# Indexer scores: two 64-row matmuls in the two halves of the array in place of two 128-row matmuls that are half zero

## Chip, cores and metric

The kernel runs on one NeuronCore of one Trainium2 chip. The metric is the device time of one execution in microseconds (us); before the change it is the median of three runs.

## What is computed

Two layers of a hybrid block on 512 tokens of width 2048. The even layer is a convolution branch beside block attention. The odd layer is an attention in which an indexer chooses the keys: for every query it scores all earlier keys with 16 small heads of 64 dimensions, and only the 128 keys with the highest scores are attended to. The part that matters here:

```python
idx = jnp.einsum('bqhd,bsd->bqhs', iq_c, ik)          # 16 heads, 64 dimensions
score = jnp.einsum('bqhs,bqh->bqs', jax.nn.relu(idx), iw_c)
score = jnp.where(kpos[None, :] <= qpos[:, None], score, -jnp.inf)
sel = lax.top_k(score, k_top)[1]                      # k_top = 128
```

## The kernel before, in words

Products are computed to nearly float32 accuracy with rounded operands: each operand is split into a high part (the value rounded to the fast matmul format, by ScalarE) and a low part (the remainder, by VectorE), and a product is the sum of high x high, high x low and low x high. `mm3` (L80 to L89) issues these three matmuls; `gemm` (L118 on) uses it for every projection, with weights that arrive by DMA in pieces and are split as they come. The work of all engines is ordered ahead of time by a planner, from the program order, due times set by `at`, and a simulated timeline.

The odd layer (`odd`, L618 on) first computes the latent queries and keys and the indexer's key `ik` (64 dimensions, 512 keys). `ik` is copied to the upper 64 partitions too, so that each half of the partitions holds it once. From it come four tiles of 128 partitions: `ihl` has the high part in the lower half and the low part in the upper half, `ilh` the other way round, `h0` has the high part below and zeros above, `zh` zeros below and the high part above (L645 to L654).

Then the 16 heads are worked off in 8 pairs. One `gemm` (L671, 384 query columns, the first 128 queries need no selection) gives the queries of two heads, one in each half of the partitions. For each head, `iq` gets the head's high part in its own half and its low part in the other half (L677, L678). For each of three chunks of 128 queries there are two matmuls into one PSUM bank, with `iq` as the weights and the keys as 256, 384 or 512 moving columns: L685 multiplies high by low and low by high in one matmul over all 128 rows, L686 multiplies high by high, with the zeros of `h0` or `zh` against the half that holds the low part. ScalarE takes the bank out with a relu (L688), and VectorE adds it, times the head's weight, into the score tile of the chunk (L690, L692). The five PSUM banks of the tags `s` and `x` are taken in turn.

After three projections ahead of the loop, four more (`gate`, L658 to L664, 16 k-steps of three matmuls) run among the head pairs, and the rest after them, while VectorE selects the 128 highest scores (L697 to L713). The attention that follows uses the selection (L238).

`colsum` (L161 to L169) sums over partitions with a matmul against ones; it is called with 64 rows and 64 columns for the indexer key's normalization.

Of the kernel before, what the change touches and what calls it, by code (L numbers as in the profile page):

```python
# [7 lines left out]
F32R = mybir.dt.float32r  # L8
I32 = mybir.dt.int32
AF = mybir.ActivationFunctionType  # L10
# [4 lines left out]
P = 128  # L15
T = 512
NT = T // P
# [9 lines left out]
KTOP = 128  # L27
# [12 lines left out]
def f32(ap):  # L40
    return ap.bitcast(F32)


class Builder:
# [573 lines left out]
    def odd(self):  # L618
        nc, d = self.nc, self.d
# [8 lines left out]
        px = self.psum("x")  # L628
# [3 lines left out]
        ik = self.s("C")  # L632
# [11 lines left out]
        lo, hi = slice(0, DI), slice(DI, P)  # L644
        ilh, ihl = self.s("T", dt=F32R), self.s("T", dt=F32R)  # L645
# [1 line left out]
        nc.scalar.activation(ilh[hi, :], ik[hi, :], AF.Copy)  # L647
        nc.vector.tensor_tensor(ilh[lo, :], ik[lo, :], f32(ihl[lo, :]), op=OP.subtract)
        nc.vector.tensor_tensor(ihl[hi, :], ik[hi, :], f32(ilh[hi, :]), op=OP.subtract)
        h0, zh = self.s("T", dt=F32R), self.s("T", dt=F32R)  # L650
        nc.vector.memset(f32(h0[hi, :]), 0.0)
        nc.vector.memset(f32(zh[lo, :]), 0.0)
        nc.scalar.activation(h0[lo, :], ik[lo, :], AF.Copy)
        nc.scalar.activation(zh[hi, :], ik[hi, :], AF.Copy)  # L654

        gates = []

        def gate():  # L658
            n = len(gates)
            ps = self.gemm(d["w_in2"][6 + n], self.xs)  # L660
            g = self.s("Y")
            nc.vector.tensor_tensor(g, ps, self.r, op=OP.mult)
            nc.scalar.activation(g, g, AF.Silu)
            gates.append(g)  # L664
# [4 lines left out]
        for i in range(HI // 2):  # L669

            ps = self.gemm(d["w_iq"][i], [(a[:, KTOP:], b[:, KTOP:]) for a, b in cq], n=T - KTOP)  # L671
            for e in range(2):
                h = 2 * i + e
                own, other = (lo, hi) if e == 0 else (hi, lo)
                iq = self.s("C", dt=F32R)
                n = T - KTOP
                nc.scalar.activation(iq[own, :n], ps[own, :n], AF.Copy)  # L677
                nc.vector.tensor_tensor(iq[other, :n], ps[own, :n], f32(iq[own, :n]), op=OP.subtract)  # L678
                cross, main = (ilh, h0) if e == 0 else (ihl, zh)
                for c in range(1, NT):  # L680
                    w = P * (c + 1)
                    cs = slice(c * P - KTOP, (c + 1) * P - KTOP)

                    px = self.psum("s" if (3 * h + c) % 5 < 2 else "x")
                    nc.tensor.matmul(px[:, :w], iq[:, cs], cross[:, :w], start=True, stop=False)  # L685
                    nc.tensor.matmul(px[:, :w], iq[:, cs], main[:, :w], start=False, stop=True)  # L686
                    rl = self.s("tmp" if (3 * h + c) % 2 else "u")
                    nc.scalar.activation(rl[:, :w], px[:, :w], AF.Relu)  # L688
                    if h == 0:
                        nc.vector.tensor_scalar(sc[c][:, :w], rl[:, :w], iw[:, c, h:h + 1], None, op0=OP.mult)  # L690
                    else:
                        nc.vector.scalar_tensor_tensor(sc[c][:, :w], rl[:, :w], iw[:, c, h:h + 1], sc[c][:, :w],  # L692
                                                       op0=OP.mult, op1=OP.add)
            self.t += 2
            if i < GI:
                gate()
# [25 lines left out]
        for pair in range(HO // 2):  # L722
# [5 lines left out]
            for b in range(2):  # L728
                ps = self.psum("g")
                for a in range(2):  # L730
                    c = 2 * b + a
                    for k in range(2):
                        cs = slice(c * P, (c + 1) * P)
# [6 lines left out]
            for e in range(2):  # L740
                h = 2 * pair + e
                th = t0 + D * e + (0 if e else 2.6)
                parts = []
                for i, (w, xs, o) in enumerate(((wk, ckv, 256 * e), ((wq0, wq1)[e], cq, 0))):
# [5 lines left out]
                    zh, zl = self.s("A2", dt=F32R), self.s("A2", dt=F32R)  # L750
# [6 lines left out]
                k, q = parts  # L757
# [159 lines left out]
```

## Time and profile before

| | |
|---|---|
| median of 3 runs | 1522.16 us (1520.82 to 1522.37) |
| profiled execution | 1521.33 us |
| its span, first to last instruction | 1519.5 us |
| mean granted TensorE clock | 0.996 |
| TensorE matmul busy | 1504.2 us, 99% of the span |
| VectorE busy | 1018.8 us, 67% |
| ScalarE busy | 677.5 us, 45% |

The span lies inside the profiled execution's time; what surrounds it is 1.8 us. The engines are named PE (TensorE matmul), PEld (TensorE weight load), DVE (VectorE), ACT (ScalarE), POOL (GpSimd) and SP (SyncE). Matmuls are pipelined and the ends of their records are modelled, so what a matmul costs is read from the start of one to the start of the next. A tile is written as weights' rows * columns, and then the moving operand.

### The profile page before, as it was taken

How to read it: one execution, taken by the hardware profiler on the slowest of the kernel's cores; microseconds unless marked ns; L12 is line 12 of the kernel's file. 1: busy time of each engine (PE TensorE's matmuls, PEld its weight loads, DVE VectorE, ACT ScalarE, POOL GpSimd, SP SyncE). 2: the span in 40 equal slices, each digit the busy share in tenths (PEclk: the TensorE clock that was granted, in tenths of full speed). 3: DMA queues.
4: the chain of work that ended last, by engine and by line, in shares of the span. 5: the costliest groups of instructions: out<-in, count | busy, mean ns of one | idle time of the engine just before them, and what ended most of it. 6: DMA issues, size and time to landing. Idle time of an engine off the chain costs nothing.

```text
span 1519.5 us, 20122 instructions
## 1 busy us (share of the span) xinstructions
PE 1504.2 (99%) x7137; PEld 1261.3 (83%) x7137; DVE 1018.8 (67%) x1980; ACT 677.5 (45%) x1219; POOL 55.5 (4%) x117
## 2 busy tenths in 40 slices
PE   9999999999999999999999999999999999999996
PEld 7888888888888888888888887788888889888886
DVE  7799999976576645664444445557995898843344
ACT  7533333345374534543333333545324666633341
POOL 0000000002022202220000000000000000000000
PEclk9999999999999999999999999999999999999998
DMA  7233333356234733364444332222232111133333
GB/s 234 89 105 114 102 106 102 104 146 173 93 108 132 204 104 115 113 173 138 146 145 145 125 98 85 95 91 78 90 98 91 55 51 49 56 125 118 126 125 112
DMA packets 97397, 173.22 MB, mean 114 GB/s; under 512 B 12112, under 2 KB 18000, under 8 KB 97296
## 3 DMA queue, kind: packets, MB, share of 16 engines
q1 hardware_dynamic: 93280, 164.45, 34.5%
q0 software_dynamic: 3584, 7.35, 1.7%
q8 instruction: 56, 0.92, 0.2%
q14 instruction: 45, 0.37, 0.1%
q10 hardware_dynamic: 432, 0.14, 0.0%
HBM read 153.93 MB, written 10.49 MB: 108 GB/s over the span
## 4 chain that ended last, share of the span: by engine, by line
PE 97%; DMA 1%; DVE 1%; ACT 0%; issue 0%; SPq 0%; DVEq 0%; ACTq 0%
PE psg L87 28%; PE psg L89 28%; PE psg L88 28%; PE psx L87 1%; PE psx L88 1%; PE psx L89 1%; PE psx L249 1%; PE pss L88 1%; PE pss L89 1%; PE pss L87 1%; PE pso L88 1%; PE pso L89 1%; PE pso L87 1%; DMA wr<-in_w_v 1%; DMA C<-in_w_in 0%; PE psx L686 0%
## 5 line engine op out<-in xcount | busy, mean ns | idle before, releaser
L96 ACT ACTIVATE wh<-wr 128x512 fp32r<-128x512 f32 x508 | 319.4, 629 | 652.2 <-PE psg L89 542.1
L97 DVE TENSOR_TENSOR wl<-wr,wh 128x512 fp32r<-128x512 f32 x508 | 348.5, 687 | 296.3 <-ACT wh L96 295.4
L87 PE MATMUL psg<-A,wh 128*128 128x512 f32 (+1 forms) x1328 | 517.0, 390 | 0.2 <-DVE tmp L782 0.2
L88 PE MATMUL psg<-A,wl 128*128 128x512 f32 x1120 | 436.5, 390 | 0.0
L89 PE MATMUL psg<-A,wh 128*128 128x512 f32 x1120 | 436.4, 390 | 0.0
L87 PEld LDWEIGHTS psg<-A,wh 128*128 128x128 f32 (+1 forms) x1328 | 248.7, 187 | 52.8 <-ACT wh L96 0.6
L88 PEld LDWEIGHTS psg<-A,wl 128*128 128x128 f32 x1120 | 209.6, 187 | 44.8 <-issue 0.4
L89 PEld LDWEIGHTS psg<-A,wh 128*128 128x128 f32 x1120 | 209.6, 187 | 44.4 <-issue 0.4
L415 DVE SCALAR_TENSOR_TENSOR C<-u,cst,C 128x512 f32<-128x512 f32 x240 | 170.0, 745 | 0.2
L89 PE MATMUL psg<-Y,wh 128*128 128x512 f32 x336 | 130.9, 390 | 0.0
L88 PE MATMUL psg<-Y,wl 128*128 128x512 f32 x336 | 130.9, 390 | 0.0
L290 POOL DMA_DIRECT2D turn<-turn x112 | 55.0, 499 | 609.0 <-DVE turn L286 459.4
L88 PEld LDWEIGHTS psg<-Y,wl 128*128 128x128 f32 x336 | 63.0, 188 | 13.0
L89 PEld LDWEIGHTS psg<-Y,wh 128*128 128x128 f32 x336 | 63.1, 188 | 12.8
L87 PE MATMUL psg<-T,wh 128*128 128x512 f32 x160 | 62.6, 391 | 0.0
L88 PE MATMUL psg<-G,wl 128*128 128x512 f32 (+1 forms) x160 | 60.7, 379 | 0.0
L89 PE MATMUL psg<-G,wh 128*128 128x512 f32 (+1 forms) x160 | 60.6, 379 | 0.0
L87 PE MATMUL psg<-Y,wh 128*128 128x512 f32 x128 | 49.8, 389 | 0.0
L240 ACT ACTIVATE C<-C,col 128x128 f32<-128x128 f32 (+1 forms) x64 | 35.8, 560 | 15.6 <-DVE col L238 15.2
L87 PE MATMUL psg<-G,wh 128*128 128x512 f32 (+1 forms) x96 | 36.2, 377 | 0.0
L87 PEld LDWEIGHTS psg<-T,wh 128*128 128x128 f32 x160 | 30.0, 188 | 6.1 <-DVE A L97 0.2
L89 PEld LDWEIGHTS psg<-G,wh 128*128 128x128 f32 x160 | 30.1, 188 | 5.1
(316 smaller groups left out, 2137.0 us busy)
## 6 DMA issues: line engine op xcount, KB each, us to landing
wr<-in_w_in SPq DMA_DIRECT2D x268, 256.0 KB, 3.0
wr<-in_w_out SPq DMA_DIRECT2D x128, 256.0 KB, 2.9
wr<-in_w_v SPq DMA_DIRECT2D x64, 256.0 KB, 2.9
wr<-in_w_qk SPq DMA_DIRECT2D x32, 256.0 KB, 2.4
turn<-turn POOLq DMA_DIRECT2D x112, 64.0 KB, 3.9
Y<-in_xT SPq DMA_DIRECT2D x16, 256.0 KB, 5.1
wr<-in_w_pw SPq DMA_DIRECT2D x16, 256.0 KB, 2.9
tmp<-in_xT SPq DMA_DIRECT2D x16, 256.0 KB, 3.0
```

Source lines behind the costliest of these rows:

```text
L87: i = mm(ps, lh, rl, start=start, stop=False)
L88: mm(ps, ll, rh, start=False, stop=False)
L89: mm(ps, lh, rh, start=False, stop=stop)
L96: i = nc.scalar.activation(th, src, AF.Copy)
L97: nc.vector.tensor_tensor(tl, src, f32(th), op=OP.subtract)
L240: nc.scalar.activation(p[:, :w], p[:, :w], AF.Exp, bias=mn, scale=-1.0, accum_out=sm)
L249: nc.tensor.transpose(px[b][:, o:o + P], p[:, j * P:(j + 1) * P], self.ident)
L290: nc.gpsimd.dma_start(y[32 * b:32 * (b + 1), a], z[32 * a:32 * (a + 1), b])
L415: nc.vector.scalar_tensor_tensor(y, u[:, i:i + T], self.c("w_dw", n * TAPS + i), y, op0=OP.mult, op1=OP.add)
```

## The change

The tiles `h0` and `zh` go, with the two clears and two copies that filled them. The two heads of a pair are worked off together, chunk by chunk. For each chunk two PSUM banks are taken, and four matmuls are issued: high x high of the first head on partitions 0 to 63, high x high of the second head on partitions 64 to 127, each with 64 rows of weights and 64 rows of keys, and then the two matmuls of 128 rows with the cross terms, one for each bank. The relu and the weighted add stay as they were, with the head's place in the pair now choosing the buffer between them.

```diff
-        h0, zh = self.s("T", dt=F32R), self.s("T", dt=F32R)
-        nc.vector.memset(f32(h0[hi, :]), 0.0)
-        nc.vector.memset(f32(zh[lo, :]), 0.0)
-        nc.scalar.activation(h0[lo, :], ik[lo, :], AF.Copy)
-        nc.scalar.activation(zh[hi, :], ik[hi, :], AF.Copy)
...
         for i in range(HI // 2):
 
             ps = self.gemm(d["w_iq"][i], [(a[:, KTOP:], b[:, KTOP:]) for a, b in cq], n=T - KTOP)
-            for e in range(2):
-                h = 2 * i + e
-                own, other = (lo, hi) if e == 0 else (hi, lo)
+            n = T - KTOP
+            iqs = []
+            for own, other in ((lo, hi), (hi, lo)):
                 iq = self.s("C", dt=F32R)
-                n = T - KTOP
                 nc.scalar.activation(iq[own, :n], ps[own, :n], AF.Copy)
                 nc.vector.tensor_tensor(iq[other, :n], ps[own, :n], f32(iq[own, :n]), op=OP.subtract)
-                cross, main = (ilh, h0) if e == 0 else (ihl, zh)
-                for c in range(1, NT):
-                    w = P * (c + 1)
-                    cs = slice(c * P - KTOP, (c + 1) * P - KTOP)
-
-                    px = self.psum("s" if (3 * h + c) % 5 < 2 else "x")
-                    nc.tensor.matmul(px[:, :w], iq[:, cs], cross[:, :w], start=True, stop=False)
-                    nc.tensor.matmul(px[:, :w], iq[:, cs], main[:, :w], start=False, stop=True)
-                    rl = self.s("tmp" if (3 * h + c) % 2 else "u")
-                    nc.scalar.activation(rl[:, :w], px[:, :w], AF.Relu)
+                iqs.append(iq)
+            for c in range(1, NT):
+                w = P * (c + 1)
+                cs = slice(c * P - KTOP, (c + 1) * P - KTOP)
+
+                px = [self.psum("s" if (6 * i + 2 * c + e) % 5 < 2 else "x") for e in range(2)]
+
+                for e, own, k in ((0, lo, ihl), (1, hi, ilh)):
+                    nc.tensor.matmul(px[e][:, :w], iqs[e][own, cs], k[own, :w], start=True, stop=False)
+                for e, k in ((0, ilh), (1, ihl)):
+                    nc.tensor.matmul(px[e][:, :w], iqs[e][:, cs], k[:, :w], start=False, stop=True)
+                for e in range(2):
+                    h = 2 * i + e
+                    rl = self.s("u" if e else "tmp")
+                    nc.scalar.activation(rl[:, :w], px[e][:, :w], AF.Relu)
```

## Rows read from the trace of the kernel before

**Rows 1.** Page, busy us by engine: share of the span, instructions.

```profile
PE 1504.2 (99%) x7137; PEld 1261.3 (83%) x7137; DVE 1018.8 (67%) x1980; ACT 677.5 (45%) x1219; POOL 55.5 (4%) x117
```

**Rows 2.** Page, the chain that ended last, by engine.

```profile
PE 97%; DMA 1%; DVE 1%; ACT 0%; issue 0%; SPq 0%; DVEq 0%; ACTq 0%
```

**Rows 3.** Table of stretches: busy us and instructions by engine, granted clock, DMA.

```profile
992.30:1069.80 77.50, 77.50 (x383) 67.67 (x382) 52.86 (x90) 43.52 (x91) 0.00 (x0) 1.00 0.27 82
1069.80:1137.00 67.20, 67.20 (x298) 55.66 (x297) 67.14 (x176) 20.10 (x33) 0.00 (x0) 1.00 0.29 96
```

**Rows 4.** Timeline, first score matmuls: start us, us, engine, line, tiles, shape, count.

```profile
992.49 0.28 PE L685 MATMUL pss<-T,C 128*128 128x256 f32 x1
992.49 0.19 PEld L686 LDWEIGHTS pss<-T,C 128*128 128x128 f32 x1
...
992.72 0.34 PE L685 MATMUL psx<-T,C 128*128 128x384 f32 x1
...
993.07 0.39 PE L685 MATMUL psx<-T,C 128*128 128x512 f32 x1
...
993.53 0.40 PE L88 MATMUL psg<-A,wl 128*128 128x512 f32 x1
```

**Rows 5.** Lines 651 and 653: duration ns min/median/max, first and last start us.

```profile
L651 DVE MEMSET T<- x1: 485/485/485, 975.9 to 975.9; 64x512 f32 x1
L653 ACT ACTIVATE T<-C x1: 632/632/632, 977.6 to 977.6; 64x512 fp32r<-64x512 f32 x1
```

**Rows 6.** Timeline around the first 64-row column sum.

```profile
957.39 0.39 PE L87 MATMUL psg<-A,wh 128*128 128x512 f32 x1
...
957.71 0.19 PEld L168 LDWEIGHTS pso<-u,one 64*64 64x64 f32 x2 [0.35 <-issue]
...
958.31 0.19 PEld L88 LDWEIGHTS psg<-A,wl 128*128 128x128 f32 x1 [0.41 <-issue]
958.31 0.51 PE L88 MATMUL psg<-A,wl 128*128 128x512 f32 x1
958.42 0.19 PEld L89 LDWEIGHTS psg<-A,wh 128*128 128x128 f32 x1
...
958.66 0.40 PE L89 MATMUL psg<-A,wh 128*128 128x512 f32 x1
```

**Rows 7.** Timeline, narrower: the second of its loads and of its matmuls.

```profile
957.76 0.13 PEld L168 LDWEIGHTS pso<-u,one 64*64 64x64 f32 x1
...
957.99 0.39 PE L168 MATMUL pso<-u,one 64*64 64x512 f32 x1
```

**Rows 8.** Timeline, the 128-row matmuls around the second 64-row column sum.

```profile
965.54 0.40 PE L88 MATMUL psg<-A,wl 128*128 128x512 f32 x1
...
966.81 0.40 PE L87 MATMUL psg<-A,wh 128*128 128x512 f32 x1
```

**Rows 9.** Timeline, weights of 80 columns, and a transpose with 80 rows.

```profile
945.63 0.39 PE L89 MATMUL psg<-A,wh 128*80 128x512 f32 x1
945.86 0.39 PE L168 MATMUL pso<-u,one 128*128 128x512 f32 x1
...
960.05 0.39 PE L89 MATMUL psg<-A,wh 128*128 128x512 f32 x1
960.06 0.14 PEld L630 LDWEIGHTS psx<-ident,C 80*128 80x128 f32 x1
960.28 0.23 PE L630 MATMUL psx<-ident,C 80*128 80x80 f32 x1
```

**Rows 10.** Timeline, end of five score pairs, and the sixth.

```profile
1009.10 0.34 PE L686 MATMUL pss<-T,C 128*128 128x384 f32 x1
...
1012.49 0.39 PE L685 MATMUL psx<-T,C 128*128 128x512 f32 x1
```

**Rows 11.** Last step of the selection, and the first read of it.

```profile
L713 DVE TENSOR_SCALAR C<-C x3: 276/354/421, 1137.2 to 1140.1; 128x256 f32<-128x256 f32 x1, 128x384 f32<-128x384 f32 x1, 128x512 f32<-128x512 f32 x1
L238 DVE CUSTOM_DVE_ANT_0 C<-pss,C x3: 414/558/692, 1169.7 to 1174.2; 128x256 f32<-128x256 f32 x1, 128x384 f32<-128x384 f32 x1, 128x512 f32<-128x512 f32 x1
```

## Prediction

> **What bounds the kernel now.** I read the busy shares first, then the chain that ended last, then a table of stretches, and only then single matmuls. TensorE is busy 99% of the span [rows 1]; the chain that ended last runs through it for 97% [rows 2]. The indexer's score matmuls all start in the stretch from 992.3 to 1069.8 us. In it TensorE is busy for all of the 77.5 us, at granted clock 1.00, which is 2.4 GHz; VectorE has 52.86 us of work in it and ScalarE 43.52 [rows 3]. So the stage costs what TensorE's stream costs, and the reader should look at starts of consecutive matmuls, not at their durations (a recorded 0.39 us matmul is followed by the next after 0.23).
>
> Two score matmuls of one width follow each other, so half of the time from one width's first start to the next is one matmul: 992.49 to 992.72 gives 0.115 us at 256 columns, 992.72 to 993.07 gives 0.175 at 384, 993.07 to 993.53 gives 0.23 at 512. A weight load starts with the matmul before it and is hidden: that of the second matmul begins at 992.49, with the first [rows 4].
>
> **The change part by part.** *Removed.* Two clears on VectorE (0.485 us the first) and two copies on ScalarE (0.632 us the first), between 975.9 and 979 us [rows 5]. TensorE then runs projections for the gates; the first score matmul starts at 992.49 [rows 4], some 13 us later. The cover is those projections, so I book 0; without cover it would be worth at most 2 x 0.485 + 2 x 0.632 = 2.2 us. The evacuations (ScalarE's relu, VectorE's weighted add), their buffers and the turn of PSUM banks stay the same in number and pattern; the two adds into one accumulator now follow each other directly. They are in any case on an engine with 25 us to spare here. No DMA and no queue is touched.
>
> *Changed on TensorE.* There are 8 head pairs with 3 query chunks each: 24 groups. A group had four matmuls of width w; it now has two of 64 rows and two of 128 rows, the same number of instructions and of weight loads.
>
> *The gain to be had.* If the two 64-row matmuls run at once in the two halves, a group loses one width: 8 x (0.115 + 0.175 + 0.23) = 4.2 us in all [rows 4]. No row shows two matmuls running at once, so this share is bounded: 0 to 4.2 us.
>
> *The price of going to 64 rows and back.* The trace has two places where 64-row matmuls stand between 128-row ones: a column sum with 64 x 64 weights, two matmuls of 512 columns each. Around the first, starts go 957.39 (128 rows), 957.71 (64, its load), 957.99 (64), 958.31 (128), 958.66 (128) [rows 6, 7]. From 957.39 to 958.66 are four matmuls of 512 columns, 1.27 us instead of 4 x 0.228 = 0.91: a round trip costs 0.36 us. The second place repeats it: 965.54 to 966.81, again 1.27 [rows 8]. It splits like this. The matmul of 957.39 has streamed by 957.62, yet the first 64-row load begins at 957.71: 0.09 of empty array. That load is not hidden: the second load begins 0.05 later, at 957.76 [rows 7]. The last 64-row matmul has streamed by 958.22, the next full load begins at 958.31: 0.09 again. That load of 128 columns is not hidden either: its follower starts 0.11 later, at 958.42 [rows 6]. So 0.09 + 0.05 + 0.09 + 0.11, with 0.02 of rounding.
>
> Is it the rows or the columns that make this? Weights of 128 rows by 80 columns run without a gap (945.63 to 945.86), and so does entry into a transpose with 80 rows (960.05 to 960.28, its load begun at 960.06 behind a running matmul) [rows 9]. So neither a smaller number of rows nor of columns is enough; 64 by 64 is. The new form, 64 rows by 128 columns, lies between. The bounds are 0 and the full round trip. I take the round trip, since 64 rows is what the new form shares with the place that paid, and since half of the array is addressed by itself, as there. The Trainium skill, TensorEngine Tiling, Tiling Modes (Key Properties), says the same against this change: a change of tiling mode drains TensorE, and it lists 64x128 as a mode beside 128x128. By the 64-row rows alone the switch is paid; by the 80-row rows alone it is not, and the sum would end at -4.2; the rule sides with the first.
>
> With 128 columns instead of 64 the first unhidden load grows from 0.05 to 0.11, so a round trip is 0.36 + 0.05 = 0.41 us; 24 of them are 9.8 us. The second 64-row load comes behind the first (the two loads at 957.71 and 957.76 followed each other), so the second matmul starts 0.11 after the first: 24 x 0.11 = 2.6 us of the overlap is lost. This is the term with the least support; its bounds are 0 and 2.6, and I take 2.6, the only order of loads that the rows show.
>
> For 24 undivided groups: 9.8 + 2.6 - 4.2 = +8.2 us.
>
> *Groups that are torn.* Six score results share five PSUM banks, so the order has a break: of the six pairs of one head pair, five run together and the sixth comes only after 14 projection matmuls (1009.10, then 1012.49 [rows 10]; the next two head pairs repeat it). In the new order positions five and six are the two heads of one chunk. Carrying over where the 48 pairs from 992.49 [rows 4] to the end of the stage now break, five groups would be torn: four at the widest chunk, one at the middle chunk. A torn group pays two round trips and overlaps nothing: 0.82, against 0.41 + 0.11 - 0.23 = 0.29 for a whole one at 512 columns. That is 0.53 more, 5 x 0.53 = 2.6 us. Bounds: no group torn (0); every group torn, 48 x 0.41 = 19.7 us in place of the whole sum.
>
> *What a later end delays.* The selection of the top scores follows on VectorE, which is busy 67.14 of the 67.2 us after the stage [rows 3]; its last step starts at 1140.1, and the first use of the result is at 1169.7 [rows 11]. That leaves 29 us, filled on TensorE by more projections, so a shift of 10 us passes through once and grows into nothing more.
>
> **Sum.** 8.2 + 2.6 = +10.8 us, against the profiled execution's 1521.3 us (span 1519.5 plus 1.8 around it): 1532.1. The median of the runs is 0.8 us above the profiled one, so I predict 1533.0.
>
> **Rivals.**
>
> *No switch is paid (faster).* If the array takes 64 rows by 128 columns as it takes 80 rows, loads stay hidden and the halves run together: -4.2 us, 1518.0. For it: both 80-wide cases in [rows 9]. Against it: the only 64-row matmuls pay in both places. It decides at a round trip of 4.2 / 24 = 0.17 us per group; above that the change loses. Chance 0.15.
>
> *Neither price nor gain.* The two halves run one after the other, with no drain: 0 us, 1522.2. For it: no row shows two matmuls at once. Chance 0.08.
>
> *The two loads side by side.* Loads into different halves do not wait for each other: 9.8 - 4.2 = +5.6 us with whole groups, 1527.8; five torn ones add a second round trip each and lose their 1.1 us of overlap, 5.6 + 2.05 + 1.1 = +8.8, 1531.0. Against it: successive loads at 957.71 and 957.76 follow in line, though both go to one place. The Trainium skill, TensorE: Matmul & The Clock Gate, Part 3 (The mechanism), has tiles of different rows start some 4 ns apart, loads overlapping; no run here shows it. Chance 0.18.
>
> *The order falls apart.* The first head's 64-row matmul needs only ScalarE's rounded half, the full ones need VectorE's remainder too, and the second head's comes later still; a planner that issues what is ready could put projection matmuls between the two. Every group torn: +19.7 us, 1541.9; half of them: 8.2 + 12 x (0.41 - 0.11 + 0.175) = +13.9, 1536.1. Against it: in the present order runs of up to five pairs stand together, with one place to break in six [rows 10]. Chance of 13 us or more: 0.12.
>
> *Forecast* (switch paid, loads in line, a few torn; +7 to +13 us, 1529 to 1535): 0.47.
>
> **How the numbers follow.** About 0.2% (3 us) is what a measurement here tells from no change. Faster takes the first rival, 0.15; same takes the second and a little beside it, 0.09; slower the rest, 0.76. The range must leave out no more than 2 in 10: I leave out the first rival and the torn cases above 16 us, and reach from 1521 to 1538. Over slower cases alone it would be 1527 to 1538.
>
> **What the profile after would show.** Right: at each group a gap of about 0.32 us from a 128-row matmul at 512 columns to the first 64-row one, the 64-row load not starting behind the matmul before it; the second 64-row matmul about 0.11 us behind the first; after the pair again some 0.09 us empty and a full load in the open; the stage from first to last score matmul some 87 us long instead of 77; the granted clock still 1.00. Wrong: loads of 64 rows that start with the matmul before them (no switch), second matmuls that start a few ns behind the first (loads side by side) or a whole width behind it (no overlap), or 64-row matmuls alone among projections (torn). A longer tail in the selection or the first attention would speak against the 29 us of cover. The forecast fails above all if 64 rows by 128 columns is no switch for the array.

## The result and the profile after

The changed kernel takes 1534.03 us (median, 1533.74 to 1534.41), the kernel before 1521.49 beside it: a ratio of 1.0085, 95% interval 1.0073 to 1.0097, 12.5 us slower. The forecast was 1533.0 us. The profiled execution has a span of 1532.4 us at a mean granted clock of 0.997.

The page after has TensorE as busy as before, 99% and on 97% of the chain, with the same 7137 matmuls, so the busy share does not show the loss [rows 1, 2]:

```profile
PE 1516.5 (99%) x7137; PEld 1259.2 (82%) x7137; DVE 1019.1 (67%) x1978; ACT 677.6 (44%) x1217; POOL 55.6 (4%) x117
...
PE 97%; DMA 1%; DVE 1%; ACT 1%; issue 0%; SPq 0%; DVEq 0%; ACTq 0%
```

The table of stretches, with the columns of [rows 3], shows where it is: the indexer's stage is 92 us long instead of 77.5, of which 11 matmuls more account for 2.5 (they are projections that moved into it; 394 against 383, at 0.23 us). The granted clock stays at 1.00 and the loads are busy for no longer than in [rows 3].

```profile
991.90:1083.90 92.00, 92.00 (x394) 67.72 (x393) 55.79 (x95) 45.02 (x90) 0.00 (x0) 1.00 0.23 74
1083.90:1150.00 66.10, 66.10 (x293) 54.70 (x292) 65.28 (x171) 19.58 (x31) 0.00 (x0) 1.00 0.28 93
```

One head alone shows the price. This is the timeline of the changed kernel, TensorE and its loads, around one 64-row matmul (L681) and its 128-row partner (L683):

```profile
998.26 0.39 PE L88 MATMUL psg<-A,wl 128*128 128x512 f32 x1
998.58 0.18 PEld L681 LDWEIGHTS psx<-T,C 64*128 64x128 f32 x1 [0.35 <-ACT wh L96]
998.58 0.49 PE L681 MATMUL psx<-T,C 64*128 64x512 f32 x1
999.00 0.19 PEld L683 LDWEIGHTS psx<-T,C 128*128 128x128 f32 x1 [0.24 <-issue]
...
999.11 0.19 PEld L89 LDWEIGHTS psg<-A,wh 128*128 128x128 f32 x1
999.34 0.40 PE L89 MATMUL psg<-A,wh 128*128 128x512 f32 x1
```

The 64-row load does not start with the matmul before it (998.26) but 0.32 us later, 0.09 after that one's columns have streamed, and it is not hidden; the way back looks the same, and its load is bare until 999.11. From 998.26 to 999.34 three matmuls of 512 columns take 1.08 us instead of 0.69: one trip to 64 rows and back costs 0.39 us. The form is 64*128, half of the rows and all of the columns, and it pays what 64*64 paid in [rows 6, 7, 8]. The load is put down to ScalarE's L96, which made the weights of a projection; the gap has the same size at the places put down to "issue", so that name explains nothing here.

What happened to the groups is seen in the timeline of TensorE's matmuls at the start of a head pair:

```profile
1024.45 0.39 PE L89 MATMUL psg<-A,wh 128*128 128x512 f32 x1
1024.77 0.38 PE L681 MATMUL psx<-T,C 64*128 64x256 f32 x1
1025.08 0.50 PE L87 MATMUL psg<-A,wh 128*128 128x512 f32 x1
...
1025.88 0.28 PE L683 MATMUL psx<-T,C 128*128 128x256 f32 x1
1025.99 0.40 PE L87 MATMUL psg<-A,wh 128*128 128x512 f32 x1
1026.23 0.40 PE L88 MATMUL psg<-A,wl 128*128 128x512 f32 x1
1026.55 0.45 PE L681 MATMUL pss<-T,C 64*128 64x256 f32 x2
1026.78 0.33 PE L681 MATMUL psx<-T,C 64*128 64x384 f32 x1
1027.04 0.56 PE L683 MATMUL pss<-T,C 128*128 128x256 f32 x2
1027.44 0.33 PE L683 MATMUL psx<-T,C 128*128 128x384 f32 x1
```

The first head's 64-row matmul stands alone among projections at 1024.77; its partner in the other half comes 1.8 us later, and there runs beside the *next chunk's* matmul (two starts at 1026.55, one line with x2). In a narrower window the second of the two stands by itself:

```profile
1026.56 0.44 PE L681 MATMUL pss<-T,C 64*128 64x384 f32 x1
```

Followed through the stage, there are 34 trips for 48 64-row matmuls, and only 6 times do two of them start together: five times a 256-column matmul beside a wider one, and once two of 512 columns, so in 23 of the 24 groups the two partners are apart. What an overlap saves is read from the same rows. From 1026.23 up to 1027.44 six matmuls start (each line with x2 holds one of 256 columns and one of 384); one after the other they would take 0.23 + 2 x 0.115 + 3 x 0.175 = 0.98 us, and they take 1.21. This trip costs 0.22 us instead of 0.39 and saves 0.17, the width of the 384 columns rather than that of the 256. Three of the overlaps save 0.17 and three 0.22, 1.2 us in all. The price and the overlap account for the loss: 34 x 0.39 = 13.3 us, less 1.2, is 12.1 us; measured 12.5, with an interval of 11.1 to 14.8.

Behind the stage nothing grew. The last step of the selection and the first read of it, each line with its first and last start, stand 29.7 us apart, against 29.6 in [rows 11]:

```profile
L712 DVE TENSOR_SCALAR C<-C x3: 285/362/432, 1150.2 to 1152.5; 128x256 f32<-128x256 f32 x1, 128x384 f32<-128x384 f32 x1, 128x512 f32<-128x512 f32 x1
...
L238 DVE CUSTOM_DVE_ANT_0 C<-pss,C x6: 415/554/692, 1182.2 to 1193.3; 128x256 f32<-128x256 f32 x2, 128x384 f32<-128x384 f32 x2, 128x512 f32<-128x512 f32 x2
```

### The profile page after: what moved, and what is told of

The parts are those of the page before. It is cut to its first block, busy times and chain, and to the rows that moved or that the text cites. A ratio compares the mean times of both kernels' runs of the same rounds, so it can differ in the third digit from the quotient of the medians.

```text
span 1532.4 us, 20100 instructions
## 1 busy us (share of the span) xinstructions
PE 1516.5 (99%) x7137; PEld 1259.2 (82%) x7137; DVE 1019.1 (67%) x1978; ACT 677.6 (44%) x1217; POOL 55.6 (4%) x117
## 4 chain that ended last, share of the span: by engine, by line
PE 97%; DMA 1%; DVE 1%; ACT 1%; issue 0%; SPq 0%; DVEq 0%; ACTq 0%
PE psg L87 27%; PE psg L88 27%; PE psg L89 27%; PE psx L87 2%; PE psx L88 2%; PE psx L89 2%; PE psx L249 1%; PE pss L88 1%; PE pss L89 1%; PE pss L87 1%; PE pso L89 1%; PE pso L88 1%; PE pso L87 1%; DMA wr<-in_w_out 1%; PE psx L683 1%; PE psx L681 1%
## 5 line engine op out<-in xcount | busy, mean ns | idle before, releaser
L96 ACT ACTIVATE wh<-wr 128x512 fp32r<-128x512 f32 x508 | 319.5, 629 | 653.2 <-PE psg L89 550.6
```

What stands on the lines that cost most here:

```text
L96: i = nc.scalar.activation(th, src, AF.Copy)
```

## The experiments

The theory to be tested: the time is 0.39 us for each trip, whatever the trip holds, less one width for each pair that runs in both halves at once. The rivals: the new order of heads and banks costs the time; the halves do not really overlap; loads follow in line.

**The new order without 64 rows.** The changed kernel's loop with the half-zero tiles of before:

```diff
...
-                for e, own, k in ((0, lo, ihl), (1, hi, ilh)):
-                    nc.tensor.matmul(px[e][:, :w], iqs[e][own, cs], k[own, :w], start=True, stop=False)
+                for e, k in ((0, h0), (1, zh)):
+                    nc.tensor.matmul(px[e][:, :w], iqs[e][:, cs], k[:, :w], start=True, stop=False)
```

> The changed kernel's loop order (both heads of a pair together, chunk by chunk) with the 128-row high x high matmuls of the kernel before, so no 64-row matmul in the indexer. Theory (every trip of the array from 128 rows to 64 and back costs about 0.39 us, the trace after has 34 of them, less about 0.8 us of overlap): no trips, so 0 +- 1 us against before, about 1521.5 us. Rival (the new order of heads, banks and buffers costs the time): it keeps the loss, about +12 us, 1534 us.

Measured: 1521.52 us, ratio 1.0002 (0.9993 to 1.0011). The order of heads, the banks and the buffers cost nothing that the interval, -1.1 to +1.7 us, would show. The loss needs the 64 rows.

**64 rows in the old order, each alone.** One line of the kernel before:

```diff
-                    nc.tensor.matmul(px[:, :w], iq[:, cs], main[:, :w], start=False, stop=True)
+                    nc.tensor.matmul(px[:, :w], iq[own, cs], main[own, :w], start=False, stop=True)
```

> The kernel before, in its own order, with the high x high matmul on the 64 rows that hold the head instead of 128 half zero: 48 64-row matmuls, each alone between 128-row ones, never two at once. Theory: 48 trips x 0.39 = +18.7 us against before, about 1540 us. Rival (what costs is the second head's load or the waiting on banks in the new order, not the trip itself): below +6 us.

Measured: 1543.71 us, ratio 1.0148 (1.0131 to 1.0165), +22.8 us instead of +18.7. The rival is out, but 4 us are more than the theory said. The table of stretches of this run (TensorE's busy time and matmuls, granted clock, DMA) has them:

```profile
1040.00:1050.00 10.00, 10.00 (x37) 0.94 0.28 83
1050.00:1055.00 5.00, 5.00 (x17) 0.79 0.11 34
1055.00:1060.00 5.00, 5.00 (x29) 1.00 0.20 71
1065.00:1070.00 5.00, 5.00 (x17) 0.92 0.16 56
1070.00:1075.00 5.00, 5.00 (x17) 0.74 0.00 0
1075.00:1080.00 5.00, 5.00 (x12) 0.60 0.15 52
1080.00:1085.00 5.00, 5.00 (x17) 0.71 0.00 0
```

Between 1040 and 1085 us the granted clock is at its lower level, 1.2 GHz, for part of the time. What it takes from these stretches is 10 x 0.06 + 5 x (0.21 + 0.08 + 0.26 + 0.40 + 0.29) = 6.8 us. The profiled execution, 1546.26 us, is 25.3 above the kernel before; 18.7 + 6.8 = 25.5. The other three have a mean clock of 0.994 to 0.995 against its 0.992, and are 2 to 4 us shorter. The timeline shows what came before one of the falls: single matmuls of 64 and 128 rows by turns, each with its load in the open (1074.17, 1074.48, 1074.80), and then their slower kind (1075.96 to 1076.65 for 512 columns):

```profile
1074.17 0.39 PE L685 MATMUL psx<-T,C 128*128 128x256 f32 x1
1074.48 0.38 PE L686 MATMUL psx<-T,C 64*128 64x256 f32 x1
1074.80 0.44 PE L685 MATMUL psx<-T,C 128*128 128x384 f32 x1
...
1075.96 0.76 PE L686 MATMUL psx<-T,C 64*128 64x512 f32 x1
1076.65 0.58 PE L685 MATMUL pss<-T,C 128*128 128x256 f32 x1
```

No other run here has a lower clock in this stage, so the fall comes with this form of the kernel. But not every series of trips brings it: from 1009.7 to 1013.2 us five single trips follow each other in the same way, and the clock stays at 1.00. What in the trips lowers it is not shown.

**What counts as another form: 64 against 96 rows.** The kernel before with fewer rows for the first head alone, the second head left at 128:

```diff
-                    nc.tensor.matmul(px[:, :w], iq[:, cs], main[:, :w], start=False, stop=True)
+                    rows = slice(0, 64) if e == 0 else slice(0, P)      # or slice(0, 96)
+                    nc.tensor.matmul(px[:, :w], iq[rows, cs], main[rows, :w], start=False, stop=True)
```

> The kernel before with the 64-row high x high matmul for the first head of each pair alone; the second head keeps 128 rows: 24 trips, none overlapped. Theory: 24 x 0.39 = +9.4 us against before, about 1531 us.

> The same with 96 rows instead of 64 for the first head (32 of them zeros). Theory (96 rows are no form of their own to the array, as 80 rows are none in the trace of before): no trips, 0 +- 1 us against before, about 1521.5 us. Rival (any matmul of less than 128 rows drains the array or bares its load): the same +9.4 us as with 64 rows.

Measured: 1530.62 us with 64 rows, ratio 1.0063 (1.0048 to 1.0078), +9.7 us; 1521.04 us with 96 rows, ratio 1.0001 (0.9991 to 1.0010). In the timeline of the run with 96 rows, the load (L687) starts with the matmul before it, and the matmul follows 0.11 us later:

```profile
991.60 0.28 PE L685 MATMUL pss<-T,C 128*128 128x256 f32 x1
991.60 0.19 PEld L687 LDWEIGHTS pss<-T,C 96*128 96x128 f32 x1
991.71 0.29 PE L687 MATMUL pss<-T,C 96*128 96x256 f32 x1
```

So fewer rows than 128 are not enough to make another form: 64 rows, half of the array, are one, and 96 are none.

**Whole groups.** The changed kernel, with the first matmul of a group waiting for all that its partner needs, and the other three kept behind it:

```diff
                 for e, own, k in ((0, lo, ihl), (1, hi, ilh)):
-                    nc.tensor.matmul(px[e][:, :w], iqs[e][own, cs], k[own, :w], start=True, stop=False)
+                    mm = nc.tensor.matmul(px[e][:, :w], iqs[e][own, cs], k[own, :w], start=True, stop=False)
+                    if e == 0:
+                        behind(mm, low, *free[0], *free[1])      # second head's low part, both banks
+                    else:
+                        self.tc.keep_in_program_order(mm)
...
```

> The changed kernel with every group of four matmuls held together: the first one waits for the second head's low part and for both banks, and the other three follow it in program order. 24 trips instead of 34, and 24 pairs side by side instead of 6. Theory: 24 x 0.39 - 4.2 = +5.2 us against before, about 1526.7 us. Rival (the halves do not really run at once, starts 4 ns apart are only how they are recorded): 24 x 0.39 = +9.4 us, about 1530.9 us. Rival (the loads follow in line, 0.11 us each, as the prediction had it): +7.8 us, about 1529.3 us.

Measured: 1526.99 us, ratio 1.0043 (1.0029 to 1.0056), +6.0 us over the 1520.95 of before beside it. The expected 1526.7 lies 0.3 away, loads in line 2.3, no overlap 3.9. By the time alone no overlap (+9.4) is out, but loads in line (+7.8) lie within the interval, +4.4 to +8.5. The trace closes that: in all 24 pairs the two matmuls start in the same hundredth of a microsecond or one apart, and so do their loads where they are shown one by one, as here (TensorE and its loads):

```profile
1050.74 0.34 PE L89 MATMUL psg<-G,wh 128*128 128x384 f32 x1
...
1051.60 0.18 PEld L695 LDWEIGHTS pss<-T,C 64*128 64x128 f32 x1 [0.84 <-DVE C L685]
1051.60 0.38 PE L695 MATMUL pss<-T,C 64*128 64x256 f32 x1 [0.52 <-DVE C L685]
1051.60 0.18 PEld L695 LDWEIGHTS psx<-T,C 64*128 64x128 f32 x1
1051.60 0.38 PE L695 MATMUL psx<-T,C 64*128 64x256 f32 x1
```

Held together, the change loses half of what it lost torn; it is still slower.

**One trip for a head pair, in both halves and in one.** All six 64-row matmuls in a row, then the six of 128 rows, on six banks. The second kernel puts the second head into the lower half too (its term is then low times high):

```diff
+            tags = {(c, e): "sxxsxo"[2 * c - 2 + e] for c in range(1, NT) for e in range(2)}
...
+            for c in range(1, NT):
+                for e, own, k in ((0, lo, ihl), (1, hi, ilh)):       # the other: (1, lo, ihl)
+                    mm = nc.tensor.matmul(px[c, e][:, :w], iqs[e][own, cs], k[own, :w], start=True, stop=False)
...
+            for c in range(1, NT):
+                for e, k in ((0, ilh), (1, ihl)):
+                    nc.tensor.matmul(px[c, e][:, :w], iqs[e][:, cs], k[:, :w], start=False, stop=True)
```

> All six 64-row matmuls of a head pair in a row, then its six 128-row ones, on six PSUM banks (one of tag o added), held together as before: 8 trips. Theory: 8 x 0.39 - 4.2 = -1.1 us against before, about 1520.4 us. Rival (no real overlap): 8 x 0.39 = +3.1 us, about 1524.6 us. Rival (the loss comes from the pair's place in the order, not from trips): no fall in proportion to the trips, still +5 us or more.

> The same as the run with one trip for a head pair, but the second head's 64-row matmul also uses the lower half of the array (it multiplies the second head's low part in place of its high part, so this term of the scores is another one). The same 8 trips and no two halves at once. Theory: 8 x 0.39 = +3.1 us against before, about 1524.6 us, 4.2 us above the run with both halves. Rival (no real overlap): the same time as the run with both halves.

Measured: 1520.51 us in both halves, ratio 0.9999 (0.9990 to 1.0008), and 1524.83 us in one, ratio 1.0029 (1.0018 to 1.0041): 4.3 us between them, where 4.2 was expected from 24 overlaps. Timeline of TensorE's matmuls, both halves:

```profile
991.82 0.39 PE L87 MATMUL psg<-A,wh 128*128 128x512 f32 x1
992.14 0.38 PE L696 MATMUL pss<-T,C 64*128 64x256 f32 x1
992.14 0.56 PE L696 MATMUL psx<-T,C 64*128 64x256 f32 x2
992.36 0.34 PE L696 MATMUL pss<-T,C 64*128 64x384 f32 x1
992.54 0.40 PE L696 MATMUL psx<-T,C 64*128 64x512 f32 x1
992.54 0.40 PE L696 MATMUL pso<-T,C 64*128 64x512 f32 x1
992.87 0.39 PE L706 MATMUL pss<-T,C 128*128 128x256 f32 x1
```

and one half:

```profile
993.43 0.39 PE L87 MATMUL psg<-A,wh 128*128 128x512 f32 x1
993.75 0.38 PE L696 MATMUL pss<-T,C 64*128 64x256 f32 x1
...
994.43 0.39 PE L696 MATMUL psx<-T,C 64*128 64x512 f32 x1
994.66 0.39 PE L696 MATMUL pso<-T,C 64*128 64x512 f32 x1
994.99 0.38 PE L706 MATMUL pss<-T,C 128*128 128x256 f32 x1
```

From the last projection to the first 128-row matmul are 1.05 us in the first and 1.56 in the second; the 0.51 between them is one head's three widths, 0.115 + 0.175 + 0.23 = 0.52. At 992.54 the two halves start on 512 columns in the same hundredth of a microsecond, in the other run 0.23 us apart. The overlap is real. The version with both halves comes out level with the kernel before: the 1.1 us that the theory gives it are within the interval, and neither shown nor refuted. No version here beats the kernel before by more than the measurement can tell.

Trips and overlaps against measured change, each with the kernel before that was measured beside it. For the change itself the price and the counts were read from its own trace, so that line is no test of the theory; the others are:

| kernel | trips | overlaps | theory, us | measured, us |
|---|---|---|---|---|
| new order, 128 rows | 0 | 0 | 0 | +0.6 |
| 96 rows, first head | 0 | 0 | 0 | +0.1 |
| one trip for a head pair | 8 | 24 | -1.1 | -0.4 |
| the same, one half | 8 | 0 | +3.1 | +3.9 |
| whole groups | 24 | 24 | +5.2 | +6.0 |
| 64 rows, first head | 24 | 0 | +9.4 | +9.7 |
| the change | 34 | 6 | +12.1 | +12.5 |
| 64 rows, each alone | 48 | 0 | +18.7 | +22.8 (clock) |

The three kernels that hold their matmuls together come out 0.7 to 0.8 us above the theory. Most of this is the price of holding: in each of the three traces, at the fifth head pair, the first 64-row matmul waits for the second head's low part, which VectorE is still writing (L685 in each). With whole groups that is the wait of 0.52 us above, and the trip costs 0.87 us where the other groups of 256 columns cost 0.27 to 0.29. With one trip for a head pair, in both halves, it is

```profile
1047.07 0.38 PE L696 MATMUL pss<-T,C 64*128 64x256 f32 x1 [0.39 <-DVE C L685]
```

and this trip costs 0.35 us, while each of the other seven saves 0.12; eight trips together save 0.5 us, against 0.4 measured. In one half the trip with the wait costs 0.87 us and the others 0.39 to 0.41.

## Why the prediction was right, and which terms were off

*The bound and the place.* Right: the stage costs TensorE's stream, and the loss sits in it: 92 us less the 2.5 of the projections that moved in is 89.5, 12 more than before. (The forecast had some 87 us there; its own sum on 77.5 gives 88.) That the removed clears and copies are worth 0 is argued, not shown, since no run leaves out them alone: in the trace before, TensorE is busy for all of the 16.4 us from 975.9 to 992.3, so it did not wait for them. The 29 us of cover behind the selection held.

*The price of a trip.* Right: 0.41 us was forecast from a 64 x 64 column sum, 0.39 measured. The choice between the 64-row and the 80-row rows [rows 6 to 9] fell on the right side; 64 rows by 128 columns is a form of its own, 96 rows by 128 is none. The Trainium skill, TensorEngine Tiling (Array Packing), Tiling Modes (Key Properties), has a change of mode drain TensorE; the trace agrees, 0.09 us empty each way.

*The second load, +2.6 us.* Wrong: the step "loads in line" fails. The two 64-row matmuls of a pair start within 0.01 us of each other, as at 992.54 above. The order of two loads into one place [rows 7] said nothing about loads into different halves; this was the term with the least support. The Trainium skill, TensorE: Matmul & The Clock Gate, Part 3 (The mechanism), has matmuls in different row groups start some 4 ns apart; the traces agree to the hundredth of a microsecond that their rows show.

*Torn groups, +2.6 us.* Far too small: only 6 overlaps are left of 24, and there are 34 trips instead of the 29 that the sum had (24 and one more for each of five). The forecast carried the old breaks over to the new positions. But the first head's 64-row matmul now needs less than its 128-row one, and stands in the planned order ahead of it, with projections between. The chip did not wait there for data: in the example above all parts of both heads were ready by 1022.5 us, 2.3 us before the first 64-row matmul. These are the last lines of ScalarE and VectorE that write them:

```profile
1021.42 0.49 ACT L671 ACTIVATE C<-psg 64x384 fp32r<-64x384 f32 x1 [0.97 <-DVE C L672]
1021.94 0.56 DVE L672 TENSOR_TENSOR C<-psg,C 64x384 fp32r<-64x384 f32 x1 [0.55 <-ACT C L671]
```

In the whole stage only two waits of weight loads for these two lines are recorded, 0.2 and 0.3 us. It is the order laid down ahead of time that tears the groups, and holding them together (24 trips) takes the loss from 12.5 to 6.0 us. That the planner's own early readiness makes that order is argued from where the matmuls stand; only that binding them removes it is shown.

That the forecast time lies within 1.0 us of the measured one is in part luck. The sum as forecast is 29 x 0.41 + 19 x 0.11 - 3.1 = 10.9; as it ran, 34 x 0.39 - 1.2 = 12.1. Five trips more add 2.0, the lower price takes off 0.6, the loads in line that did not come take off 2.1, and the overlap that was lost adds 1.9: the wrong terms had opposite signs. The kernel before also ran 0.7 us lower beside the change than the forecast had it, so the change itself was missed by 1.7 us (+10.8 forecast, +12.5 measured). What happened is two of the rivals together: the order fell apart, with 23 groups of 24 torn where the forecast had five, and the loads went side by side where two 64-row matmuls met. The first cost less than the 19.7 us of its rival because 64-row matmuls of different groups shared trips, 34 instead of 48, and six times overlapped.

## What to carry to other kernels

Count trips, not idle rows: where the stream around is of 128 rows, a visit to half of the array costs about 0.4 us, and two halves at once give back one matmul's columns (0.12 to 0.23 us here), so at these widths a single pair does not pay, and several pairs must share a trip; three pairs in one trip came out level here, not faster. Look for the price in the trace that is already there, in any small matmul of the same kind. And when matmuls must stand next to each other to be worth anything, say so to the planner: what is ready earlier is otherwise issued earlier, alone.

## What the runs show of the hardware

- With 48 single trips the granted clock fell to 0.60 in the stretch from 1075 to 1080 us though TensorE counted as busy all the time, and the clock took 6.8 us from the profiled execution. With 34 trips it stayed at 1.00.
- 96 rows of weights cost the same as 128: a ratio of 1.0001 (0.9991 to 1.0010).
- Matmuls of unlike width from two heads, 256 columns in one half and 384 in the other, also start together (the two at 1026.55 in the changed kernel); the overlap does not need partners of one group.
